# Two merges' gate projections by Strassen's block product, with the operand sums made on VectorE, ScalarE and GpSimd

## The chip, the cores and the metric

The kernel runs on one core of a Trainium2 chip. The core has a matrix engine (TensorE, PE in the rows, with its weight loads as PEld), VectorE (DVE), ScalarE (ACT), GpSimd (POOL) and SyncE (SP), each with its own in-order queue of instructions. The metric is the device time of one launch in microseconds (us); lower is better.

## The reference

One layer of a hybrid decoder block on x of 512 tokens by 1,024 channels, in float32. Four mixers read the same normalised input h; each result is projected and gated, and the four are summed:

```python
h = rmsnorm(x, norm_pre[l])
u = h @ w_in[l]                      # 1024 x 9,000-odd columns; the last 4096 are the merge gates
branches = (gdn_branch(...), gla_branch(...), ssd_branch(...), nsa_branch(...))
gates = jax.nn.sigmoid(_cols(u, offs, 'merge_gate', 'merge_gate')).reshape(bsz, s_len, 4, D_MODEL)
merged = jnp.zeros((bsz, s_len, D_MODEL), F32)
for n, y in enumerate(branches):
    merged = merged + gates[:, :, n] * (y @ w_br[l, n])
out = merged @ w_out[l]
x = x + rmsnorm(out, norm_post[l])
```

What matters here is `gates`: for each branch n, a product of a 1024x1024 weight with the transposed h (1024 channels by 512 tokens).

## The kernel before

**Products.** Every product is made of split operands: a float32 value is held as a high part and a low part (`hhi`/`hlo` for h, `wh`/`wl` for a weight, `yh`/`yl` for a branch's result), and `mm3` issues three matmuls for each block: wh with hhi, wh with hlo, wl with hhi. A weight tile of 128x1024 comes by DMA into `ws` (three buffers); ScalarE casts it into `wh`, VectorE subtracts `wl = ws - wh` (two buffers each). All of this is in `wload`.

**Stages.** The work is recorded stage by stage in the order of the list `ORDER`: the mixers `gdn`, `nsa`, `gla`, `ssd` and the merges `m0` (gdn), `m3` (nsa), `m1` (gla), `m2` (ssd). Then a list scheduler (`Sched`) places each recorded instruction on its engine's queue, by costs of its own and by free buffers of the pools (34 general buffers of 128x512 tagged `g`, 12 larger ones, 3 `ws`, 2 `wh`, 2 `wl`, 3 `mth` buffers, and in PSUM 3 banks `big` and 5 smaller uses). Stages overlap: products of the merge `m3` fill TensorE while the chains of the mixer `ssd` wait. All engine instructions are issued from one line (519), so rows are told apart by the names of their tiles.

**A merge.** `merge(n)` goes over four pairs of 128-channel blocks. A pair has two gate projections (`proj_ft`: 24 matmuls each of 128 weight rows by 512 tokens into one PSUM bank), then the branch's own product for the same two blocks (12 matmuls of 512 columns each). The gate goes through tanh on ScalarE into `mth`, VectorE forms (mth + 1) times the branch product in place, and GpSimd adds it to `merged`:

```python
th = S.buf("mth", [P, T], F32, 'cv')
act.activation(th, psg, AF.Tanh, scale=0.5)
...
dve.scalar_tensor_tensor(th, th, 1.0, ps, op0=OP.add, op1=OP.mult)
m_ops.append(pool.tensor_add(merged[d], merged[d], th))
```

**The end of `ssd`.** For each of four token tiles GpSimd adds the two parts of y (`y<-y,yo`), VectorE multiplies by the gate (`yz<-y,z`), ScalarE sums squares, VectorE and GpSimd make the reciprocal root (`yss`, `yrstd`), VectorE scales `yz` (`yz<-yz,yrstd,onc`), and TensorE transposes it with four matmuls `p_ssd<-ident,yz`. On TensorE these stand inside the products of `m3`, at places that the scheduler chose; TensorE's queue is in order, so a late `yz` holds up the products behind it.

After the merges `merged` is split into `hhi`/`hlo` once more and goes through `w_out` (matmuls `tf` of 256 columns, token rows out), the last norm and the residual.

Of the kernel before, what the change touches and what calls it, by code (L numbers as in the profile page):

```python
# [7 lines left out]
F32 = mybir.dt.float32  # L8
# [7 lines left out]
P = 128  # L16
# [25 lines left out]
NG = 34  # L42
N4 = 12
GPAIR = 0
ORDER = ('gdn', 'nsa', 'gla', 'm0', 'ssd', 'm3', 'm1', 'm2')

# [550 lines left out]
def block_kernel(ctx, tc, a, out):  # L599
# [131 lines left out]
    dskip = bcast_row('d_skip_c', 8)  # L731


    def wload(srcs, cut, shape, res=(), group=True):

        if group:
            S.grp += 1
        st, hi, lo = (S.buf(nm, [P, 1024], dt, nm).rearrange(cut, **shape)
                      for nm, dt in (('ws', F32), ('wh', F32R), ('wl', F32R)))
        o = 0  # L740
        for i, src in enumerate(srcs):
            n = src.shape[-1]
            op = sp.dma_start(st[:, :, o:o + n], src)
            if i == 0:
                op.resv = [v.buf for v in res]
            loads.append(op)
            o += n
        early = len(loads) <= 2
        S.urgent = 0 if early else -1
        c = act.copy(hi, st)  # L750
        t = (pool if early else dve).tensor_sub(lo, st, f32(hi))
        S.urgent = None
        if early:

            c.key, t.key = (0, xload.prio[1] + 40), (0, xload.prio[1] + 41)
        return hi, lo, op
# [926 lines left out]
            dve.scalar_tensor_tensor(z[c], opair, 0.5, z[c], op0=OP.mult, op1=OP.mult)  # L1683


    merged, m_ops = [None] * ND, []

    def merge(n):
        y = ytiles[n]
        yh, yl, ready = Feat("yh", F32R), Feat("yl", F32R), []  # L1690
        for b in range(4):
            ready.append(act.copy(yh[b], y[b]))
            ready.append(pool.tensor_sub(yl[b], y[b], f32(yh[b])))
        for d2 in range(ND // 2):
            ds = (2 * d2, 2 * d2 + 1)
            first = merged[ds[0]] is None
            if first:
                for d in ds:
                    merged[d] = w2("merged")
            ths = []  # L1700
            for i, d in enumerate(ds):
                psg = proj_ft(OFF['merge_gate'] + n * D + d * P, *([merged[v] for v in ds] if first and i == 0 else []),
                              group=i == 0)
                if i == 0:
                    for e in ready:
                        S.order(loads[-1], e)
                th = S.buf("mth", [P, T], F32, 'cv')
                act.activation(th, psg, AF.Tanh, scale=0.5)
                ths.append(th)
            src = a['w_br'][0, n][:, d2 * 256:(d2 + 1) * 256].rearrange("(b p) f -> p b f", p=P)  # L1710
            hi, lo, _ = wload([src], "p (b f) -> p b f", dict(f=256), group=False)
            for i, d in enumerate(ds):
                th = ths[i]
                ps = big()
                for b in range(4):
                    fs = slice(i * P, (i + 1) * P)
                    mm3(ps, hi[:, b, fs], lo[:, b, fs], yh[b], yl[b], b == 0, b == 3)
                if first:
                    dve.scalar_tensor_tensor(merged[d], th, 1.0, ps, op0=OP.add, op1=OP.mult)
                else:  # L1720
                    dve.scalar_tensor_tensor(th, th, 1.0, ps, op0=OP.add, op1=OP.mult)
                    m_ops.append(pool.tensor_add(merged[d], merged[d], th))

    stages = dict(gdn=gdn, nsa=nsa, ssd=ssd, gla=gla, m0=lambda: merge(0), m1=lambda: merge(1), m2=lambda: merge(2),
                  m3=lambda: merge(3))
    for i, stage in enumerate(ORDER):
        S.rank = i + 1
# [79 lines left out]
```

## Time and profile before

| | |
|---|---|
| median of 3 runs | 832.19 us (831.02 to 832.38) |
| the profiled execution: its time, its span | 830.03 us, 828.3 us |
| busy share: TensorE, VectorE, ScalarE, GpSimd | 97%, 60%, 45%, 25% |
| mean granted TensorE clock | 0.995 |

The span is the time from the first to the last instruction of the profiled execution; its device time is 1.73 us longer. Busy shares are shares of the span; a matmul's row has its own duration, and neighbouring matmuls overlap, so the step from one start to the next is what TensorE pays for one.

### The profile page before, as it was taken

To read this page: it belongs to the slowest core of one execution; us is meant where nothing else is said; L and a number is where in the kernel's file an instruction comes from. 1 tells how busy PE (TensorE), PEld (TensorE's weight loads), DVE (VectorE), ACT (ScalarE), POOL (GpSimd) and SP (SyncE) were. 2 spreads that over 40 slices of the span, in tenths; PEclk is the share of its full clock that TensorE was granted. 3 is DMA by queue.
4 is the path that set the end of the run, shared out by engine and by line. 5 is a ranking of instruction groups with operands and counts; after the bars stand their busy time and mean duration, and the time that the engine had idled before them with its cause. 6 is when DMAs were issued, how large, how long until landed. Compare 5 with 4: busy or idle time off the path is not lost.

```text
span 828.3 us, 12822 instructions
## 1 busy us (share of the span) xinstructions
PE 804.7 (97%) x4772; PEld 674.8 (81%) x4772; DVE 500.2 (60%) x1112; ACT 373.7 (45%) x878; POOL 204.7 (25%) x254
## 2 busy tenths in 40 slices
PE   5999999999999999999999899999999999999996
PEld 5888887897888899888887677898888888888996
DVE  5687766576535777777765977657633433343635
ACT  5444723323345767676554734635422222222432
POOL 6000263240231322222222500215521311121101
PEclk9999999999999999999999999999999999999998
DMA  7434254510132121211212221433133333334242
GB/s 231 89 104 127 77 135 104 128 27 2 51 102 76 52 53 52 77 52 51 77 51 77 52 77 51 115 105 100 51 102 87 92 102 102 81 98 127 94 162 102
DMA packets 112742, 72.39 MB, mean 87 GB/s; under 512 B 11788, under 2 KB 108232, under 8 KB 112680
## 3 DMA queue, kind: packets, MB, share of 16 engines
q1 hardware_dynamic: 111976, 69.86, 30.6%
q0 software_dynamic: 704, 1.70, 0.8%
q8 instruction: 38, 0.62, 0.3%
q14 instruction: 24, 0.20, 0.1%
HBM read 68.12 MB, written 3.43 MB: 86 GB/s over the span
## 4 chain that ended last, share of the span: by engine, by line
PE 88%; DVE 4%; ACT 2%; issue 2%; DMA 1%; POOL 1%; POOLq 0%; SPq 0%; DVEq 0%; ACTq 0%
PE big L519 58%; PE tf L519 11%; PE p_nsa L519 8%; PE p_gdn L519 5%; PE p_gla L519 2%; PE p_ssd L519 2%; DMA xt<-in_x 1%; DMA rows<-scrG 1%; PE p_head_tail L519 1%; DVE wl L519 0%; DVE gb L519 0%; POOL se L519 0%; ACT sq L519 0%; ACT wh L519 0%; DVE cv L519 0%
## 5 line engine op out<-in xcount | busy, mean ns | idle before, releaser
L519 DVE TENSOR_TENSOR wl<-ws,wh 128x1024 fp32r<-128x1024 f32 x108 | 147.9, 1369 | 161.3 <-ACT wh L519 160.1
L519 PE MATMUL big<-hlo,wh 128*128 128x512 f32 (+1 forms) x632 | 243.8, 393 | 0.0
L519 PE MATMUL big<-hhi,wh 128*128 128x512 f32 (+2 forms) x632 | 243.8, 393 | 0.0
L519 PE MATMUL big<-hhi,wl 128*128 128x512 f32 (+1 forms) x624 | 239.9, 392 | 0.0
L519 ACT CAST wh<-ws 128x1024 fp32r<-128x1024 f32 (+1 forms) x111 | 115.8, 1044 | 247.7 <-PE big L519 201.6
L519 PEld LDWEIGHTS big<-hhi,wh 128*128 128x128 f32 (+1 forms) x632 | 117.0, 188 | 25.6 <-issue 0.4
L519 PEld LDWEIGHTS big<-hlo,wh 128*128 128x128 f32 x632 | 116.3, 187 | 25.7 <-issue 0.6
L519 PEld LDWEIGHTS big<-hhi,wl 128*128 128x128 f32 x624 | 115.3, 188 | 25.1 <-issue 0.8
L519 PE MATMUL tf<-wl,hhi 128*128 128x256 f32 x288 | 81.0, 282 | 0.0
L519 PE MATMUL tf<-wh,hlo 128*128 128x256 f32 x288 | 80.9, 282 | 0.0
L519 PE MATMUL tf<-wh,hhi 128*128 128x256 f32 x288 | 80.9, 282 | 0.0
L519 POOL TENSOR_SCALAR se<-se,r,ngate 128x128 f32<-128x128 f32 (+1 forms) x64 | 41.5, 649 | 153.8 <-DVE r L519 121.0
L519 POOL TENSOR_TENSOR merged<-merged,mth 128x512 f32<-128x512 f32 x24 | 33.2, 1383 | 147.4 <-DVE mth L519 147.4
L519 PEld LDWEIGHTS tf<-wl,hhi 128*128 128x128 f32 x288 | 54.1, 188 | 0.4
L519 PEld LDWEIGHTS tf<-wh,hhi 128*128 128x128 f32 x288 | 54.0, 188 | 0.5
L519 PEld LDWEIGHTS tf<-wh,hlo 128*128 128x128 f32 x288 | 54.0, 188 | 0.4
L519 PE MATMUL big<-yl,wh 128*128 128x512 f32 x128 | 50.4, 394 | 0.0
L519 PE MATMUL big<-yh,wh 128*128 128x512 f32 x128 | 50.2, 392 | 0.0
L519 PE MATMUL big<-yh,wl 128*128 128x512 f32 x128 | 50.1, 392 | 0.0
L519 ACT ACTIVATE se<-se,mn 128x128 f32<-128x128 f32 (+1 forms) x64 | 36.1, 564 | 24.0 <-DVE mn L519 22.8
L519 DVE SCALAR_TENSOR_TENSOR cv<-big,cols,cv 128x511 f32<-128x511 f32 (+2 forms) x60 | 44.6, 743 | 1.5 <-ACT cv L519 0.5
L519 DVE CUSTOM_DVE_ANT_0 se<-p_nsa,nb 128x128 f32<-128x128 f32 (+1 forms) x64 | 30.9, 482 | 8.2 <-PE p_nsa L519 7.8
(335 smaller groups left out, 1240.4 us busy)
## 6 DMA issues: line engine op xcount, KB each, us to landing
ws<-in_w_in SPq DMA_DIRECT2D x84, 512.0 KB, 3.8
ws<-in_w_br SPq DMA_DIRECT2D x16, 512.0 KB, 3.5
ws<-in_w_out SPq DMA_DIRECT2D x8, 512.0 KB, 3.5
rows<-scrG SPq DMA_DIRECT2D x12, 256.0 KB, 4.8
xt<-in_x SPq DMA_DIRECT2D x4, 512.0 KB, 3.5
xr<-in_x SPq DMA_DIRECT2D x4, 512.0 KB, 4.4
out<-xo SPq DMA_DIRECT2D x8, 256.0 KB, 2.7
scrA<-B POOLq DMA_DIRECT2D x4, 256.0 KB, 3.1
```

Of the source, the lines that this page charges most:

```text
L519: return fn(*[res(v) for v in args], **{k: res(v) for k, v in kw.items()})
```

## The change

Between `m3` and `m1` a new stage `sums` is recorded; `m1` and `m2` then make the gate projections of a pair in `gate_pair`, in place of two calls of `proj_ft`. The weight of a pair is seen as two by two blocks A (two blocks of 128 gate channels, two halves of the 1024 input channels), h as two by two blocks B (two halves of the input channels, two halves of the 512 tokens). Strassen's form (in Winograd's variant) needs seven block products in place of eight:

- A11·B11, A12·B21, S1·T1, S2·T2, S3·T3, S4·B22 and A22·T4, each of 4 x 3 matmuls of 256 columns: 84 matmuls of 256 columns in place of 48 of 512.
- The sums S1 to S4 of weight blocks are made in each pair (four VectorE instructions of 128x512), and each of the seven left operands is split by a cast (ScalarE) and a subtraction (VectorE) of 128x512.
- The sums T1 to T4 of h are made once, in `sums`: for each of two groups four GpSimd additions `hx<-hhi,hlo`, four VectorE subtractions among the `hx`, four ScalarE casts and four VectorE subtractions for the low parts. T3 is written over the quarter of `hhi`/`hlo` that it replaces, so it waits for the last product of `m3`.
- The results are put together from two PSUM banks `fa` and `fb` with a copy `p15` (ScalarE, 128x512 from PSUM) and five VectorE additions of 256 columns; the second block of the tanh is taken in halves.

The branch's weight is cast and split in two halves. The loads are the same three of 512 KB per pair. `m0` and `m3` stay as they were.

```diff
...
-ORDER = ('gdn', 'nsa', 'gla', 'm0', 'ssd', 'm3', 'm1', 'm2')
+ORDER = ('gdn', 'nsa', 'gla', 'm0', 'ssd', 'm3', 'sums', 'm1', 'm2')
...
     dskip = bcast_row('d_skip_c', 8)
-    def wload(srcs, cut, shape, res=(), group=True):
+    def wload(srcs, cut, shape, res=(), group=True, halves=False):
...
             o += n
         early = len(loads) <= 2
         S.urgent = 0 if early else -1
-        c = act.copy(hi, st)
-        t = (pool if early else dve).tensor_sub(lo, st, f32(hi))
+        na = hi.arr.shape[0]
+        for r in ([slice(0, na // 2), slice(na // 2, na)] if halves else [slice(0, na)]):
+            c = act.copy(hi[:, r], st[:, r])
+            t = (pool if early else dve).tensor_sub(lo[:, r], st[:, r], f32(hi[:, r]))
         S.urgent = None
         if early:
...
             dve.scalar_tensor_tensor(z[c], opair, 0.5, z[c], op0=OP.mult, op1=OP.mult)
+    HT = T // 2
+    mov, sum_ops = {}, []
+    def sums():
+        c1, c2 = slice(0, HT), slice(HT, T)
+        ts = {n: [w2(f"T{n}{p}", None, F32R).rearrange("p (a b) -> p a b", b=HT) for p in "hl" for _ in range(2)]
+              for n in (1, 2, 4)}
+        for j in range(2):
+            k1, k2 = slice(2 * j, 2 * j + 2), slice(4 + 2 * j, 6 + 2 * j)
+            x11, x12, x21, x22 = (w2("hx").rearrange("p (a b) -> p a b", b=HT) for _ in range(4))
+            for x, k, c in ((x12, k1, c2), (x11, k1, c1), (x22, k2, c2), (x21, k2, c1)):
+                S.order(pool.tensor_add(x, f32(hhi[:, k, c]), f32(hlo[:, k, c])), loads[-7])
+            dve.tensor_sub(x11, x12, x11)
+            dve.tensor_sub(x12, x22, x12)
+            dve.tensor_sub(x22, x22, x11)
+            dve.tensor_sub(x21, x21, x22)
+            for n, x in ((1, x11), (2, x22), (4, x21), (3, x12)):
+                hi, lo = (ts[n][j], ts[n][2 + j]) if n != 3 else (hhi[:, k1, c2], hlo[:, k1, c2])
+                act.copy(hi, x)
+                sum_ops.append(dve.tensor_sub(lo, x, f32(hi)))
+        for n in (1, 2, 4):
+            mov['T', n] = [(ts[n][k // 2][:, k % 2], ts[n][2 + k // 2][:, k % 2]) for k in range(4)]
+        for n, k0, c in ((11, 0, c1), (21, 4, c1), (22, 4, c2)):
+            mov['B', n] = [(hhi[:, k0 + k, c], hlo[:, k0 + k, c]) for k in range(4)]
+        mov['T', 3] = [(hhi[:, k, c2], hlo[:, k, c2]) for k in range(4)]
+    def gate_pair(c0, res):
+        S.grp += 1
+        ws = []
+        s1, s2, s3, s4 = (w2(f"S{i}") for i in range(1, 5))
+        p15, u23 = w2("p15"), w2("u23")
+        for i in range(2):
+            st = S.buf("ws", [P, 1024], F32, 'ws')
+            op = sp.dma_start(st.rearrange("p (a f) -> p a f", f=P),
+                              W[:, c0 + i * P:c0 + (i + 1) * P].rearrange("(a p) f -> p a f", p=P))
+            if i == 0:
+                op.resv = [v.buf for v in (*res, s1, s2, s3, s4, p15, u23)]
+                for e in sum_ops:
+                    S.order(op, e)
+            loads.append(op)
+            ws.append(st)
+        first_load = loads[-2]
+        h1, h2 = slice(0, 512), slice(512, 1024)
+        a11, a12, a21, a22 = ws[0][:, h1], ws[0][:, h2], ws[1][:, h1], ws[1][:, h2]
+        S.urgent = -1
+        dve.tensor_add(s1, a21, a22)
+        dve.tensor_sub(s2, s1, a11)
+        dve.tensor_sub(s3, a11, a21)
+        dve.tensor_sub(s4, a12, s2)
+        S.urgent = None
+        parts = {}
+        for pair in ((('A', 11, a11), ('S', 1, s1)), (('S', 2, s2), ('A', 12, a12)), (('S', 3, s3), ('S', 4, s4)),
+                     (('A', 22, a22),)):
+            hi, lo = (S.buf(nm, [P, 1024], F32R, nm) for nm in ('wh', 'wl'))
+            for i, (nm, n, src) in enumerate(pair):
+                r = slice(i * 512, i * 512 + 512)
+                S.urgent = -1
+                act.copy(hi[:, r], src)
+                dve.tensor_sub(lo[:, r], src, f32(hi[:, r]))
+                S.urgent = None
+                parts[nm, n] = [v[:, r].rearrange("p (a f) -> p a f", f=P) for v in (hi, lo)]
+        fa, fb = big(), big()
+        l, r = slice(0, HT), slice(HT, T)
+        def product(ps, a_, b_, start):
+            (hi, lo), ms = parts[a_], mov[b_]
+            for k in range(4):
+                mm3(ps, hi[:, k], lo[:, k], *ms[k], start and k == 0, k == 3, True)
+        th1, th2 = (S.buf("mth", [P, T], F32, 'cv') for _ in range(2))
+        product(fa[:, l], ('A', 11), ('B', 11), True)
+        product(fa[:, r], ('S', 1), ('T', 1), False)
+        act.copy(p15, fa)
+        product(fb[:, l], ('S', 2), ('T', 2), True)
+        dve.tensor_add(u23[:, l], fb[:, l], p15[:, l])
+        product(fa[:, l], ('A', 12), ('B', 21), False)
+        product(fb[:, l], ('S', 3), ('T', 3), False)
+        dve.tensor_add(u23[:, r], fb[:, l], p15[:, l])
+        product(fa[:, r], ('S', 4), ('B', 22), False)
+        act.activation(th1[:, l], fa[:, l], AF.Tanh, scale=0.5)
+        dve.tensor_add(th1[:, r], fa[:, r], u23[:, l])
+        act.activation(th1[:, r], th1[:, r], AF.Tanh, scale=0.5)
+        product(fb[:, l], ('A', 22), ('T', 4), False)
+        dve.tensor_add(th2[:, l], fb[:, l], p15[:, l])
+        dve.tensor_add(th2[:, r], u23[:, r], p15[:, r])
+        act.activation(th2, th2, AF.Tanh, scale=0.5)
+        return [th1, th2], first_load
     merged, m_ops = [None] * ND, []
     def merge(n):
...
                 for d in ds:
                     merged[d] = w2("merged")
             ths = []
-            for i, d in enumerate(ds):
-                psg = proj_ft(OFF['merge_gate'] + n * D + d * P, *([merged[v] for v in ds] if first and i == 0 else []),
-                              group=i == 0)
-                if i == 0:
-                    for e in ready:
-                        S.order(loads[-1], e)
-                th = S.buf("mth", [P, T], F32, 'cv')
-                act.activation(th, psg, AF.Tanh, scale=0.5)
-                ths.append(th)
+            if mov:
+                ths, ld = gate_pair(OFF['merge_gate'] + n * D + d2 * 256, [merged[v] for v in ds] if first else ())
+                for e in ready:
+                    S.order(ld, e)
+            else:
+                for i, d in enumerate(ds):
+                    psg = proj_ft(OFF['merge_gate'] + n * D + d * P, *([merged[v] for v in ds] if first and i == 0 else []),
+                                  group=i == 0)
+                    if i == 0:
+                        for e in ready:
+                            S.order(loads[-1], e)
+                    th = S.buf("mth", [P, T], F32, 'cv')
+                    act.activation(th, psg, AF.Tanh, scale=0.5)
+                    ths.append(th)
             src = a['w_br'][0, n][:, d2 * 256:(d2 + 1) * 256].rearrange("(b p) f -> p b f", p=P)
-            hi, lo, _ = wload([src], "p (b f) -> p b f", dict(f=256), group=False)
+            hi, lo, _ = wload([src], "p (b f) -> p b f", dict(f=256), group=False, halves=bool(mov))
             for i, d in enumerate(ds):
                 th = ths[i]
                 ps = big()
...
                     dve.scalar_tensor_tensor(th, th, 1.0, ps, op0=OP.add, op1=OP.mult)
                     m_ops.append(pool.tensor_add(merged[d], merged[d], th))
-    stages = dict(gdn=gdn, nsa=nsa, ssd=ssd, gla=gla, m0=lambda: merge(0), m1=lambda: merge(1), m2=lambda: merge(2),
+    stages = dict(gdn=gdn, nsa=nsa, ssd=ssd, gla=gla, sums=sums, m0=lambda: merge(0), m1=lambda: merge(1), m2=lambda: merge(2),
                   m3=lambda: merge(3))
     for i, stage in enumerate(ORDER):
         S.rank = i + 1
```

On VectorE, at the end of `ssd` (names as above; `T1l` is the low part of T1; rows that begin with + are new):

```order
 L519 TENSOR_SCALAR yss<-yss 128x1
 L519 SCALAR_TENSOR_TENSOR rows<-rows,cb 128x512
+L519 TENSOR_TENSOR hx<-hx 128x512
+L519 SCALAR_TENSOR_TENSOR mth<-mth,big 128x512
 L519 SCALAR_TENSOR_TENSOR yz<-yz,yrstd,onc 128x512
+L519 TENSOR_TENSOR y<-p_ssd,xD 128x512
+L519 TENSOR_TENSOR hx<-hx 128x512 x2
+L519 SCALAR_TENSOR_TENSOR yo<-p_ssd,egc 128x512
+L519 TENSOR_TENSOR hx<-hx 128x512
+L519 TENSOR_TENSOR T1l<-hx,T1h 128x512
 L519 SCALAR_TENSOR_TENSOR mth<-mth,big 128x512
```

The fourth tile's `yz<-y,z` comes next but one behind these rows, then `T2l`, `T4l`, `yss`, two more `hx`, and the scaled `yz`; before, no `hx` and no `T` stood between. On TensorE the four transposes of that last `yz` stood behind 19 matmuls of the second last gate of their pair, and now stand behind six of the gate after it.

On GpSimd at the same place (`yl` is the low part of the nsa and ssd results, `yrstd` the reciprocal root):

```order
-L519 TENSOR_TENSOR yl<-z,yh 128x512 x2
+L519 TENSOR_TENSOR hx<-hhi,hlo 128x512 x2
 L519 TENSOR_TENSOR y<-y,yo 128x512
+L519 TENSOR_TENSOR hx<-hhi,hlo 128x512 x3
 L519 TENSOR_TENSOR yrstd<-yss,negh 128x1
+L519 TENSOR_TENSOR hx<-hhi,hlo 128x512
 L519 TENSOR_TENSOR merged<-merged,mth 128x512
+L519 TENSOR_TENSOR hx<-hhi,hlo 128x512
 L519 TENSOR_TENSOR y<-y,yo 128x512
+L519 TENSOR_TENSOR hx<-hhi,hlo 128x512
 L519 TENSOR_TENSOR merged<-merged,mth 128x512
```

Eight additions came in; the two `yl` moved behind the second `merged`.

On ScalarE in a pair of `m1` of the changed kernel (`S_6640` to `S_6643` are S1 to S4 of one pair, `p_6644` is `p15`):

```order
+L519 CAST wh<-S_6640 128x512
+L519 ACTIVATE mth<-mth 128x512
+L519 CAST wh<-S_6641 128x512
+L519 CAST wh<-ws 128x512
+L519 CAST wh<-S_6642 128x512
+L519 CAST wh<-S_6643 128x512
+L519 COPY p_6644<-big 128x512
+L519 CAST wh<-ws 128x512 x3
+L519 ACTIVATE mth<-big 128x256
```

Before, a pair had three casts of 128x1024 and two tanh of 128x512; the copy `p15` now stands behind the casts of S3 and S4.

## Rows read from the trace of the kernel before

**Rows 1.** The page: busy time of the engines, and the chain by engine.

```profile
PE 804.7 (97%) x4772; PEld 674.8 (81%) x4772; DVE 500.2 (60%) x1112; ACT 373.7 (45%) x878; POOL 204.7 (25%) x254
...
PE 88%; DVE 4%; ACT 2%; issue 2%; DMA 1%; POOL 1%; POOLq 0%; SPq 0%; DVEq 0%; ACTq 0%
```

**Rows 2.** Stretch, us: busy time of PE, PEld, DVE, ACT, POOL, clock.

```profile
650.00:700.00 50.00, 50.00 (x218) 40.47 (x217) 18.55 (x16) 12.43 (x16) 7.71 (x6) 1.00 0.35 95
```

**Rows 3.** Timeline of PE: start us, duration us; a pair of `m2`.

```profile
742.91 0.39 PE L519 MATMUL big<-hhi,wh 128*128 128x512 f32 x1
...
754.11 0.39 PE L519 MATMUL big<-yh,wh 128*128 128x512 f32 x1
...
759.57 0.39 PE L519 MATMUL big<-hhi,wh 128*128 128x512 f32 x1
```

**Rows 4.** Timeline of PE: matmuls of 256 columns.

```profile
18.30 1.07 PE L519 MATMUL big<-hhi,wl 128*128 128x256 f32 x8
20.11 1.07 PE L519 MATMUL big<-hlo,wh 128*128 128x256 f32 x8
...
779.76 0.28 PE L519 MATMUL tf<-wh,hhi 128*128 128x256 f32 x1
...
794.72 0.28 PE L519 MATMUL tf<-wl,hhi 128*128 128x256 f32 x1
```

**Rows 5.** Timeline of ACT: casts behind each other.

```profile
766.58 3.67 ACT L519 CAST hhi<-merged 128x512 fp32r<-128x512 f32 x6
775.86 0.62 ACT L519 CAST hhi<-merged 128x512 fp32r<-128x512 f32 x1 [3.58 <-POOL merged L519]
776.39 1.05 ACT L519 CAST wh<-ws 128x1024 fp32r<-128x1024 f32 x1
```

**Rows 6.** Groups by form: busy us, mean ns of one, idle before.

```profile
L519 ACT ACTIVATE mth<-big 128x512 f32<-128x512 f32 x32 | 18.9, 591 | 0.0
L519 DVE TENSOR_TENSOR hlo<-merged,hhi 128x512 fp32r<-128x512 f32 x8 | 5.1, 681 | 0.0
```

**Rows 7.** Timeline of DVE and POOL where they meet, and DVE alone.

```profile
605.21 1.23 DVE L519 TENSOR_TENSOR wl<-ws,wh 128x1024 fp32r<-128x1024 f32 x1 [3.99 <-ACT wh L519]
...
610.68 2.35 DVE L519 TENSOR_TENSOR wl<-ws,wh 128x1024 fp32r<-128x1024 f32 x1
610.67 1.29 POOL L519 TENSOR_TENSOR merged<-merged,mth 128x512 f32<-128x512 f32 x1 [1.50 <-DVE mth L519]
...
593.11 1.23 DVE L519 TENSOR_TENSOR wl<-ws,wh 128x1024 fp32r<-128x1024 f32 x1
593.17 2.32 POOL L519 TENSOR_TENSOR merged<-merged,mth 128x512 f32<-128x512 f32 x1 [1.40 <-DVE mth L519]
...
573.04 1.04 POOL L519 TENSOR_TENSOR xdd<-xdt,eld 128x512 f32<-128x512 f32 x1
573.45 1.18 DVE L519 TENSOR_TENSOR yz<-y,z 128x512 f32<-128x512 f32 x1
```

**Rows 8.** Timelines at the end of `ssd`: POOL, DVE, PE.

```profile
581.45 1.29 POOL L519 TENSOR_TENSOR y<-y,yo 128x512 f32<-128x512 f32 x1
...
583.14 0.68 DVE L519 TENSOR_TENSOR yz<-y,z 128x512 f32<-128x512 f32 x1
...
592.05 0.39 PE L519 MATMUL big<-hhi,wh 128*128 128x512 f32 x1
...
596.25 0.40 PE L519 MATMUL big<-hhi,wh 128*128 128x512 f32 x1
596.93 0.63 PE L519 MATMUL p_ssd<-ident,yz 128*128 128x128 f32 x4 [0.29 <-DVE yz L519]
```

**Rows 9.** PE at a gap, and the granted clock (PEclk) behind it.

```profile
474.09 0.49 PE L519 MATMUL p_gla<-qe,ke 64*128 64x128 f32 x4 [2.47 <-DVE ke L519]
...
476.00:477.00 1.00, 1.00 (x8) 0.41 (x8) 1.00 (x3) 0.75 (x2) 0.00 (x0) 0.50 0.00 0
479.00:480.00 1.00, 1.00 (x5) 0.75 (x4) 0.92 (x2) 0.95 (x2) 0.00 (x0) 0.97 0.55 137
```

## The prediction

> **What bounds the kernel now.** I read the page first: TensorE is busy 97% of the span, and the chain of work that ended last runs over TensorE for 88% of it [rows 1]. Then the windows by stage: in the merges after `ssd` TensorE is busy 50.00 of 50 us at a clock of 1.00, while VectorE works 18.55, ScalarE 12.43 and GpSimd 7.71 us [rows 2]. So there a microsecond of matmuls removed is a microsecond won, as long as the three helpers, with 30 us and more to spare in 50, deliver in time. The timeline of one pair of blocks gives the price: 48 gate matmuls of 512 columns from 742.91 to 754.11, 11.20 us or 233.3 ns each, then 24 of the branch to 759.57, 5.46 us; a pair is 16.66 us [rows 3]. `m1` and `m2` have eight such pairs.
>
> **The matmuls.** A pair's gates become 84 matmuls of 256 columns. That is 7/8 of the columns, but in 1.75 times the instructions, so the step of a 256-column matmul decides; break-even is 11.20/84 = 133 ns. Two places show steps: 16 matmuls from 18.30 to 20.11, 113 ns, and 127 steps from 779.76 to 794.72, 117.8 ns [rows 4]. Their weights change with each matmul, as here. I take half the gate's step, 116.7 ns, which lies between: a product of 12 is 1.40 us, seven are 9.80, and the raw gain is 1.40 us a pair (1.30 by the slower row, 1.68 by the faster).
>
> The Trainium skill ("TensorE: Matmul & The Clock Gate", Back-to-back issue gap) states 262 cycles at 2.4 GHz for 256 columns and 518 for 512, 109 and 216 ns; by it seven products would be an estimated 9.2 us. The 233.3 ns of the trace speak against using it here, since a gate's matmul takes 17 ns longer than that.
>
> **A pair's helpers.** VectorE gets four S sums, seven low parts and two halves of the branch's low part, 13 of 128x512 at 0.68 us [rows 6], 8.9 us; five additions of 256 columns (between half of 0.68 and all of it, about 0.45 each) 2.2 us; and the two products with mth as before, about 1.4 us: 12.5 us in a pair of about 15.7. ScalarE gets nine casts, the copy and tanh: about 8 us (casts 0.61, tanh 0.59 [rows 5, 6]). Both fit on the average; what matters is order. In ScalarE's queue the copy p15 stands behind the casts of S3 and S4, and these need a `wh` buffer (there are two) that S1·T1 is still reading. Call X the end of S1·T1. The two casts and the copy end 0.05 + 2 x 0.53 + 0.6 = 1.73 us after X if casts follow each other as at 775.86 and 776.39, and 1.9 us if as the six from 766.58, 3.67 us together [rows 5]. A12·B21 adds into the half of the bank that p15 reads, so it can't start before; its nominal start is X + 1.40. TensorE waits 0.37 to 0.55 us in each pair; I take 0.4. What comes late next is S3·T3, with operands cast long before, so nothing builds up. The weight loads are the same three per pair, and earlier than needed. The period is then 9.80 + 0.40 + 5.46 = 15.66 us, a gain of 1.0 us a pair, **8.0 us** for eight (7.2 by the slower step of rows 4, 10.4 by the faster without change of the wait).
>
> **Entry to m1.** The first pair has no pair ahead to hide behind: its four sums stand on VectorE behind the last-but-one `mth` product of `m3`, which needs half of the branch products, 2.7 us after the last gate of `m3` ends, and 0.2 more, and then three instructions and the split of A11 follow, partly against a GpSimd addition. I count VectorE done at 7.1 us after that gate, and TensorE through the branch products at 5.5 to 5.9: **1.5 us** lost (0 to 2.5).
>
> **The sums.** This term decides the sign. `sums` puts eight GpSimd additions, eight VectorE subtractions, eight casts and eight more subtractions beside the end of `ssd`. None of them is on TensorE, and VectorE and GpSimd have idle time there. But the rows show that the two don't work beside each other. The split `wl` takes 1.23 us alone and 2.35 us when it starts 0.01 us behind a GpSimd addition of 1.29 us; the same addition started 0.06 us behind a `wl` takes 2.32; `yz<-y,z` takes 1.18 beside `xdd` and 0.68 alone [rows 7, 8]. In each case the later one ends a full instruction behind the end of the earlier: 0.55 us for a VectorE instruction of 128x512, 1.08 for one of 1024, 1.15 for the GpSimd addition. So instructions of both with operands in SBUF go one by one, in turns. All sixteen VectorE instructions of `sums` and all eight additions are of that kind.
>
> The Trainium skill ("SBUF — State Buffer", Who interferes with whom) has this as a rule: a VectorE instruction with two inputs in SBUF shares a read port with GpSimd, and whoever issues first holds it to its end. By that rule the sums aren't hidden but queue up; the trace agrees, 2.35 us against 1.23.
>
> Now the queues as the change orders them. GpSimd's eight additions stand ahead of the second `merged`, six of them behind the `y` that starts at 581.45 and ends at 582.75 [rows 8]. From there to the last scaled `yz` the exclusive work is: on GpSimd six additions, one y and two merged, 9 x 1.15 = 10.4 us; on VectorE 15 instructions of 128x512 (among them nine of `sums`), 8.3 us, and two `wl`, 2.2 us. That is 20.9 us, so `yz` can't be done before 603.7. VectorE's four instructions that read PSUM (4 x 0.6 us) need no turn but hold their queue, and GpSimd's `yrstd` stands between VectorE's `yss` and the scaled `yz`; stepping through both queues in turns these add some 4 us, and I get 607.7. Before, `yz` let TensorE go on at 596.93, after a wait of 0.29 us [rows 8].
>
> TensorE reaches these transposes later than before in the program: six matmuls into the next gate. Its own way there is already held up twice (`rows` is late by 1.9 and 1.1 us, since it waits in VectorE's queue, and the third tile's `yz` by 1.1, partly overlapping), so the gate that began at 592.05 [rows 8] starts at about 594.3, and the transposes are reached at 601.3. They wait until 607.7: 6.4 us. Before, the same place in the program was passed at about 600.0; after, at 608.2. **8.2 us late**, with 4 (if `yz` is done at 603.7) and 10 as bounds.
>
> A wait of that length costs the clock too. The one comparable gap of the trace, 2.47 us of idle TensorE up to 474.09, is followed by a granted clock at half of 2.4 GHz (0.50) in three slices of 1 us from 476 on, and part of a fourth, back to 0.97 at 479 to 480 [rows 9]. About 3.4 us at half speed cost **1.7 us** (0 if the gap is short).
>
> The casts and low parts of T3 come after the last gate of `m3` and are counted in the entry. The end of the kernel is as before.
>
> **Sum.** Against the profiled execution of before, 830.03 us: + 8.2 + 1.7 + 1.5 - 8.0 = 833.4. The median of the runs stands 2.16 us higher (832.19), so I forecast **835.6 us**. A difference of 0.2%, 1.7 us, is about what a measurement of this kernel can tell from no change.
>
> **Rivals.**
> *The sums hide after all* (faster). If GpSimd's additions run early, in the gaps that it has before 581.45, or if the yz chain gets ahead of them, TensorE isn't held and only the entry is lost: 832.19 + 1.5 - 8.0 = 825.7. It decides where `yz` is ready by 601.3. For it speak GpSimd's idle time; against it that its queue is in order, and all eight additions stand behind `ssd`'s own instructions, six of them behind the y of 581.45 [rows 8]. Chance 0.22.
> *Half of it* (same). The wait is 3 to 4 us, the clock is kept or half lost: 832.19 + 4 + 0.8 + 1.5 - 8.0 = 830.5, up to 833.8. Chance 0.23.
> *VectorE becomes the bound of a pair* (slower than forecast). 12.5 us and two additions of GpSimd that lock it out, 2 x 1.29, are 15.1 of 15.7; with the waits for ScalarE between, a pair could last 16.2. The gain is then 3.7 and the time 839.9. For it speaks the alternation; against it that half of VectorE's work is needed only late in a pair. Chance 0.13.
> *256 columns cost 133 ns or more*, so that Strassen saves nothing: 843.6. No row shows such a step. Chance 0.02.
> The forecast has the remaining 0.40.
>
> **Range.** From 826.0 to 840.5. Below lies the better half of the first rival; above, the bound of 10 us together with the slower step, and what is worse than 839.9 in the third: together under 0.2. By themselves the forecast's own bounds are 831 to 839. Faster by over 0.2% are the first rival and a little of the second, 0.25; within 0.2% most of the second and a little of the forecast, 0.21; slower the rest, 0.54.
>
> **What the changed profile would show.** The gate stretch of a pair at 9.8 us for 84 matmuls, steps near 117 ns, and a pair at 15.7; a wait of 0.4 us ahead of A12·B21 that ends with p15; at the end of `ssd` VectorE and GpSimd instructions of 128x512 at up to twice their length, a TensorE wait of some 6 us released by VectorE's `yz`, and PEclk at 0.5 for some 3 us behind it; a wait of about 1.5 us ahead of the first A11·B11. The prediction is wrong if `yz` comes early (no long wait), if a pair's period isn't near 15.7, or if the transposes stand elsewhere than at the place where TensorE comes first.

## The result, and the profile after

The changed kernel takes 837.9 us (median of 4 runs, 837.52 to 839.0) against 832.08 us: a ratio of 1.0085 (95% interval 1.0071 to 1.0100; the two medians alone give 1.0070). The forecast of 835.6 us lies 2.3 us below; its direction held, its size didn't. The profiled execution took 837.55 us, 7.5 us more than that of before, where the forecast had 3.4. The page's line of busy times and the chain by engine:

```profile
PE 800.5 (96%) x5060; PEld 685.9 (82%) x5060; DVE 574.9 (69%) x1248; ACT 401.0 (48%) x950; POOL 224.0 (27%) x262
...
PE 82%; DVE 10%; ACT 3%; issue 2%; DMA 1%; POOL 1%; POOLq 0%; DVEq 0%; SPq 0%; ACTq 0%
```

TensorE is busy 4 us less than before [rows 1], in a span 7.5 us longer: matmuls were saved, and more than that was lost in waits. The chain now runs over VectorE for 10%. What TensorE waited for from 560 to 790 us (engine and tile, releaser: us in all, times, longest):

```profile
PE p_ssd L519 <- DVE yz L519: 5.4, 1, 5.4
PE big L519 <- DVE wl L519: 3.3, 1, 3.3
PE p_ssd L519 <- issue: 2.4, 3, 1.4
PE big L519 <- ACT p L519: 1.5, 7, 0.2
```

Three places, then: the last `yz` of `ssd`, the first low part `wl` of m1, and the copy `p15` in seven of the eight pairs. The three waits put down to the issue (2.4 us) stand ahead of the products `p_ssd<-xdt,rows` of `ssd`; one of 0.7 was there before. First the end of `ssd`, in the timelines of GpSimd, VectorE and TensorE (start us, duration us):

```profile
582.01 4.65 POOL L519 TENSOR_TENSOR hx<-hhi,hlo 128x512 f32<-128x512 f32 x3
...
582.45 1.41 DVE L519 TENSOR_TENSOR yz<-y,z 128x512 f32<-128x512 f32 x1
583.78 1.76 DVE L519 SCALAR_TENSOR_TENSOR rows<-rows,cb 128x512 f32<-128x512 f32 x1
585.46 2.28 DVE L519 TENSOR_TENSOR wl<-ws,wh 128x1024 fp32r<-128x1024 f32 x1
...
604.50 1.75 DVE L519 SCALAR_TENSOR_TENSOR yz<-yz,yrstd,onc 128x512 f32<-128x512 f32 x1
...
606.39 1.09 PE L519 MATMUL p_ssd<-ident,yz 128*128 128x128 f32 x4 [5.44 <-DVE yz L519]
...
608.13 0.63 PE L519 MATMUL big<-hhi,wl 128*128 128x512 f32 x1
608.56 0.63 PE L519 MATMUL big<-hhi,wh 128*128 128x512 f32 x1
...
611.04 0.39 PE L519 MATMUL big<-hlo,wh 128*128 128x512 f32 x1
```

GpSimd's three `hx` take 4.65 us, 1.55 each, and beside them `yz` takes 1.41, `rows` 1.76 and `wl` 2.28 us; alone, `yz` took 0.68 and `wl` 1.23 [rows 7, 8]. The last scaled `yz` is done at 606.25; TensorE waits 5.44 us for it, and then takes 0.43 us from one matmul of 512 columns to the next until 0.23 returns. The windows show why (us, then busy time of PE, PEld, DVE, ACT and POOL; the number behind POOL's count is the granted clock):

```profile
604.00:605.00 1.00, 0.00 (x0) 0.00 (x0) 1.00 (x2) 1.00 (x2) 1.00 (x2) 0.50 0.00 0
609.00:610.00 1.00, 1.00 (x4) 0.81 (x3) 1.00 (x2) 0.72 (x2) 1.00 (x1) 0.50 0.76 199
610.00:611.00 1.00, 1.00 (x5) 0.82 (x4) 1.00 (x2) 0.00 (x0) 1.00 (x2) 0.79 0.92 324
```

Within the wait the granted clock falls to 0.50, and it comes back only behind 610. TensorE reaches m1 at 651.68, against 642.95 before. All work of this run stood 0.69 us earlier than in the run of before when `ssd` came to its last steps, so the loss there is 9.4 us. The rows for this are two of the kernel before and one of the changed kernel:

```profile
576.18 1.97 PE L519 MATMUL p_ssd<-xdt,rows 128*128 128x64 f32 x16 [0.67 <-issue]
642.95 0.39 PE L519 MATMUL big<-hhi,wh 128*128 128x512 f32 x1
...
575.49 1.97 PE L519 MATMUL p_ssd<-xdt,rows 128*128 128x64 f32 x16 [0.68 <-issue]
```

Then the entry to m1, the same three engines:

```profile
650.00 1.67 POOL L519 TENSOR_TENSOR merged<-merged,mth 128x512 f32<-128x512 f32 x1 [12.65 <-DVE mth L519]
651.63 3.38 POOL L519 TENSOR_TENSOR yl<-yT,yh 128x512 fp32r<-128x512 f32 x2
...
649.23 0.69 DVE L519 SCALAR_TENSOR_TENSOR mth<-mth,big 128x512 f32<-128x512 f32 x1 [4.27 <-PE big L519]
649.84 2.38 DVE L519 TENSOR_TENSOR S<-ws 128x512 f32<-128x512 f32 x2
652.15 1.75 DVE L519 TENSOR_TENSOR S<-S,ws 128x512 f32<-128x512 f32 x1
653.81 1.75 DVE L519 TENSOR_TENSOR wl<-ws,wh 128x512 fp32r<-128x512 f32 x1
...
651.68 0.28 PE L519 MATMUL big<-hhi,wh 128*128 128x256 f32 x1
...
655.62 0.58 PE L519 MATMUL big<-hhi,wl 128*128 128x256 f32 x1 [3.30 <-DVE wl L519]
...
661.54 0.32 PE L519 MATMUL big<-T2l,wh 128*128 128x256 f32 x1
...
673.42 0.28 PE L519 MATMUL big<-hhi,wh 128*128 128x256 f32 x1
```

The weight sums S stand behind `mth`, start at 649.84, and meet three GpSimd additions in a row: `merged` and two `yl`. The third sum and the first `wl` behind it take 1.75 us each instead of 0.7. TensorE begins m1 at 651.68, issues four matmuls, waits 3.30 us, and then goes at half clock, 0.21 us a matmul of 256 columns, until 661.54. The first pair lasts to 673.42, 21.74 us.

The other seven pairs, here the last:

```profile
767.97 0.28 PE L519 MATMUL big<-hhi,wh 128*128 128x256 f32 x1
...
772.63 0.38 PE L519 MATMUL big<-hhi,wh 128*128 128x256 f32 x1 [0.21 <-ACT p L519]
...
778.24 0.40 PE L519 MATMUL big<-yh,wh 128*128 128x512 f32 x1
...
783.74 0.28 PE L519 MATMUL tf<-wh,hhi 128*128 128x256 f32 x1
```

From 767.97 to 778.24 the gates take 10.27 us. The last matmul ahead of the gap started at 772.13, 0.50 us before that of 772.63, so 0.38 us of this are the wait and the 84 matmuls took 9.89; with the branch a pair takes 15.77 us. Before it took 16.66 [rows 3].

### The profile page after: what moved, and what is told of

It reads as the page before. It is cut to its first block, busy times and chain, and to the rows that moved or that the text cites. A ratio compares the mean times of both kernels' runs of the same rounds, so it can differ in the third digit from the quotient of the medians.

```text
span 835.8 us, 13677 instructions
## 1 busy us (share of the span) xinstructions
PE 800.5 (96%) x5060; PEld 685.9 (82%) x5060; DVE 574.9 (69%) x1248; ACT 401.0 (48%) x950; POOL 224.0 (27%) x262
## 4 chain that ended last, share of the span: by engine, by line
PE 82%; DVE 10%; ACT 3%; issue 2%; DMA 1%; POOL 1%; POOLq 0%; DVEq 0%; SPq 0%; ACTq 0%
PE big L519 52%; PE tf L519 11%; PE p_nsa L519 8%; PE p_gdn L519 5%; DVE wl L519 3%; PE p_gla L519 2%; PE p_ssd L519 2%; DVE mth L519 1%; ACT wh L519 1%; DMA xt<-in_x 1%; DVE yz L519 1%; DVE hx L519 1%; PE p_head_tail L519 1%; DMA rows<-scrG 1%; DVE S L519 0%
## 5 line engine op out<-in xcount | busy, mean ns | idle before, releaser
L519 PE MATMUL big<-hhi,wh 128*128 128x512 f32 (+2 forms) x632 | 231.5, 374 | 1.6 <-ACT p L519 1.5
L519 PE MATMUL big<-hlo,wh 128*128 128x512 f32 (+1 forms) x632 | 229.5, 371 | 0.0
L519 PE MATMUL big<-hhi,wl 128*128 128x512 f32 (+1 forms) x624 | 225.8, 369 | 3.3 <-DVE wl L519 3.3
L519 DVE TENSOR_TENSOR wl<-ws,wh 128x1024 fp32r<-128x1024 f32 (+1 forms) x124 | 146.8, 1190 | 104.6 <-ACT wh L519 104.3
L519 ACT CAST wh<-ws 128x1024 fp32r<-128x1024 f32 (+2 forms) x127 | 114.6, 909 | 173.3 <-PE big L519 125.7
L519 POOL TENSOR_TENSOR merged<-merged,mth 128x512 f32<-128x512 f32 x24 | 36.3, 1525 | 139.6 <-ACT mth L519 90.1
```

The lines of the kernel that those rows point to most:

```text
L519: return fn(*[res(v) for v in args], **{k: res(v) for k, v in kw.items()})
```

## The experiments

All ratios are to the kernel before, run on the same chip beside them. Since the work ahead of the sums ended 0.7 us earlier to 1.8 us later than in the run of before, the loss at the end of `ssd` is counted from a row that they all have (the sixteen matmuls `p_ssd<-xdt,rows` at 575 to 578 us) to the first matmul of m1, less the same of before: 9.4 us for the changed kernel. Each experiment has one trace, and the executions of one kernel lie up to 6 us apart (830.76 to 836.94 in the ten of VectorE's sums held back). This stretch, left as it was, lost 9.4 us in the changed kernel, 9.8 in "weight sums first" and 10.1 in "the copy sooner"; differences of that size between two traces show nothing.

My theory at this point: VectorE and GpSimd go in turns, so the sums hold up the `yz` chain; the entry is held by the place of the weight sums in VectorE's queue; the pairs by the place of `p15` in ScalarE's. The rivals: queue length alone at the end of `ssd`; a late weight load at the entry; VectorE's subtractions in a pair.

**GpSimd writes only.**

```diff
-                S.order(pool.tensor_add(x, f32(hhi[:, k, c]), f32(hlo[:, k, c])), loads[-7])
+                S.order(pool.memset(x, 0.5, _r=[f32(hhi[:, k, c]), f32(hlo[:, k, c])]), loads[-7])
+                S.ops[-1].cost = 1227.0
+                pool.memset(x, 0.5)
+                S.ops[-1].cost = 1.0
```

> The changed kernel with each of the eight GpSimd additions hx = hhi + hlo replaced by two writes of a constant into the same buffer, about as long together, which read nothing from SBUF; so the T sums are not those of h. The order on TensorE, VectorE and ScalarE is the same to the row. Theory (VectorE and GpSimd go in turns when both read SBUF): the VectorE instructions beside the writes take 0.68 us instead of 1.4 to 1.8, the last scaled yz is done some 6 us sooner, TensorE's wait of 5.4 us ahead of the last transposes falls below 1.5 us and the half clock behind it goes; the time falls from 837.6 by 7 to 9 us, to about 829 to 831. Rival (the queues are simply too long: nine more VectorE instructions ahead of yz, and GpSimd as busy as before): yz comes at most 2 us sooner and the time stays above 835.

Measured: ratio 1.0040 (1.0023 to 1.0057), profiled execution 834.56 us, 3.0 less than the changed kernel's. GpSimd, VectorE and TensorE at the end of `ssd`:

```profile
582.61 3.10 POOL L519 MEMSET hx<- 128x512 f32 x6
...
583.29 0.68 DVE L519 TENSOR_TENSOR yz<-y,z 128x512 f32<-128x512 f32 x1
584.63 1.23 DVE L519 TENSOR_TENSOR wl<-ws,wh 128x1024 fp32r<-128x1024 f32 x1
...
595.76 1.77 DVE L519 TENSOR_TENSOR yz<-y,z 128x512 f32<-128x512 f32 x1
...
601.24 1.76 DVE L519 SCALAR_TENSOR_TENSOR yz<-yz,yrstd,onc 128x512 f32<-128x512 f32 x1
...
603.14 1.09 PE L519 MATMUL p_ssd<-ident,yz 128*128 128x128 f32 x4 [3.79 <-DVE yz L519]
```

Beside the six writes from 582.61 the first `yz` and `wl` take what they take alone, though GpSimd is busy without a break there. So the doubling comes from two engines reading, not from GpSimd being busy; that part of the theory holds. The Trainium skill ("SBUF — State Buffer", Who interferes with whom) draws the same line: a VectorE instruction with two inputs in SBUF contends with a GpSimd instruction that reads SBUF, not with one that only writes it; 0.68 us beside the writes agrees. But only 3 us came back, and 6.1 of the 9.4 us stay: the wait is still 3.79 us, and the half clock is there. The expectation failed, and the run doesn't separate queue length from turns, since GpSimd's own `merged`, `y` and `yl` still read: from 589 to 603 us six VectorE rows, the last two `yz` among them, take some 5 us more than alone. Two of these GpSimd instructions are the `yl<-z,yh` that the change moved from 579 us to a place beside `T2l` and the last `yz`; no run puts them back.

**VectorE's sums held back**, the counterpart (run later, shown here): the GpSimd additions as they are, the subtractions behind the last `yz`.

```diff
-            dve.tensor_sub(x11, x12, x11)
+            S.order(dve.tensor_sub(x11, x12, x11), loads[-4])
```

> The changed kernel with the GpSimd additions where they are (same rows, same order up to the second merged) but VectorE's subtractions among the hx, and so the T parts, held back to loads[-4], behind the last yz. The counterpart to the run in which GpSimd only wrote: there 4.1 of some 10 us by which yz was late came back. Theory (both halves count: GpSimd's reads, and nine more instructions in VectorE's queue): the GpSimd additions alone still make VectorE's own yz, rows and wl wait their turn, some 2 to 4 us of the 9.5 stay, time 831 to 834 against 837.6, with rows of 1.2 to 1.8 us on VectorE beside hx. Rival (VectorE's own queue is all that counts): the wait ahead of the last transposes is under 0.5 us and TensorE reaches m1 as early as without sums, time below 829.5.

Measured: ratio 1.0035 (1.0018 to 1.0052), profiled execution with 5.6 of the 9.4 us still lost. VectorE, then TensorE:

```profile
583.02 1.41 DVE L519 TENSOR_TENSOR yz<-y,z 128x512 f32<-128x512 f32 x1
...
596.63 2.31 DVE L519 TENSOR_TENSOR wl<-ws,wh 128x1024 fp32r<-128x1024 f32 x1
...
601.55 0.63 PE L519 MATMUL p_ssd<-ident,yz 128*128 128x128 f32 x4 [1.99 <-DVE yz L519]
...
602.92 0.63 PE L519 MATMUL big<-hlo,wh 128*128 128x512 f32 x1
```

VectorE's own `yz` and `wl` still wait their turn (1.41, 2.31 us). The loss that stays is more than the expected 2 to 4 us, though the median, 833.64 us, lies in the range that was named, and the rival (below 829.5) falls: 5.6 us are lost here without any of VectorE's sums. So with either half gone 5.6 to 6.1 us stay in the trace, of 9.4; each pays for the clock: after a wait of only 1.99 us the matmuls take 0.43 us as well, from 602.49 to 605.90. Whether the two halves add isn't shown: the traces give back 3.3 and 3.8 us, together less than 9.4, but by the ratios it is 3.7 and 4.2 us, each within some 2 us, together no less than the 7.3 us that moving both brings (below).

**No sums.** The seven products read blocks of h in place of T1 to T4.

```diff
     def sums():
         c1, c2 = slice(0, HT), slice(HT, T)
+        for n, k0, c in ((1, 0, c2), (2, 4, c2), (3, 0, c2), (4, 4, c1)):
+            mov['T', n] = [(hhi[:, k0 + k, c], hlo[:, k0 + k, c]) for k in range(4)]
...
+        return
```

> The changed kernel without the stage sums: the seven products read blocks of h in place of T1 to T4, so the gates are not the reference's; matmuls, weight sums and the putting together stay. Theory: the loss at the end of ssd (9.5 us by comparing when TensorE reaches m1) goes, the pairs keep 15.76 us against 16.66, and the entry to m1 keeps part of its 6.0 us: 837.6 - 9.5 = 828 if the entry is unchanged, 825 if the entry shrinks with the earlier load. Rival (the sums matter little and the pairs themselves don't gain): not below 832.

Measured: ratio 0.9926 (0.9906 to 0.9947), profiled execution 822.97 us, median 825.13. TensorE reaches m1 as in the kernel before (within 0.1 us), a pair takes 15.7 us, and the entry has no wait at all: the load is no longer ordered behind T3, and the sums S begin at 634.34, 9.4 us ahead of m1's first matmul. That is the lower of the two expected times: part of the entry's cost is the sums' too. The rival falls.

**Sums only**, with the gates of m1 and m2 plain.

```diff
-            if mov:
+            if False:
...
-            hi, lo, _ = wload([src], "p (b f) -> p b f", dict(f=256), group=False, halves=bool(mov))
+            hi, lo, _ = wload([src], "p (b f) -> p b f", dict(f=256), group=False, halves=False)
```

> The changed kernel with the gates of m1 and m2 plain again (two proj_ft per pair) but with the stage sums, whose T1, T2 and T4 nobody reads; since T3 is written over a quarter of h, the gates of m1 and m2 are not the reference's. It prices the sums by themselves. Theory (all of the 9.5 us at the end of ssd is the sums' own): slower than before by 9 to 10 us, ratio 1.0105 to 1.012, with a TensorE wait of over 5 us ahead of the last transposes. Rival (part of that loss comes from the Strassen pairs, whose loads and buffers reach back into m3): at most 5 us slower.

Measured: ratio 1.0126 (1.0111 to 1.0141), 10.5 us and so a little above what was expected; 10.1 of them lie at the end of `ssd`. The wait ahead of the last transposes was 3.9 us (expected over 5), the rest shorter waits ahead of it and the half clock, here twice: from 588 to 596 us already, behind a wait of 1.36 us, and again behind the long wait. The sums' price is their own, and the rival falls.

**Weight sums first.** The last two `mth` products of m3 are ordered behind S4 of the first pair.

```diff
-        dve.tensor_sub(s4, a12, s2)
+        o4 = dve.tensor_sub(s4, a12, s2)
+        if res_first[0]:
+            res_first[0] = False
+            for e in stts[-2:]:
+                S.order(e, o4)
...
-                    dve.scalar_tensor_tensor(th, th, 1.0, ps, op0=OP.add, op1=OP.mult)
+                    stts.append(dve.scalar_tensor_tensor(th, th, 1.0, ps, op0=OP.add, op1=OP.mult))
```

> The changed kernel, with the two last products mth of m3 on VectorE held back behind the weight sums S1 to S4 of the first pair of m1 (and so their GpSimd additions). Theory (the entry costs 6.0 us since the sums stand behind mth, which waits for TensorE, and then meet GpSimd's additions): the sums run about 3 us sooner and alone, the wait of 3.3 us ahead of the second half of A11 B11 falls below 0.5 us, the clock stays whole there, and the time falls by 4 to 6 us to about 832 to 833.5. Rival (the weight load comes too late, so the place in the queue does not matter): less than 1.5 us.

Measured: ratio 1.0045 (1.0029 to 1.0061), profiled execution 833.58 us, 4.0 less than the changed kernel's, at the edge of what was expected; the median of its five runs is 835.24. VectorE at the entry, where m1 begins at 652.57:

```profile
645.77 1.29 DVE L519 TENSOR_TENSOR S<-ws 128x512 f32<-128x512 f32 x2
646.97 0.69 DVE L519 TENSOR_TENSOR S<-S,ws 128x512 f32<-128x512 f32 x1
648.51 0.69 DVE L519 TENSOR_TENSOR wl<-ws,wh 128x512 fp32r<-128x512 f32 x1 [0.85 <-ACT wh L519]
```

The sums now begin 6.8 us ahead of m1's first matmul instead of 1.8, and take some 0.65 us each; so the load wasn't late, and the rival falls. They start earlier and also meet no GpSimd addition; the run takes both away at once. What TensorE waited for that it had not waited for in the changed kernel:

```profile
PE big L519 <- DVE u L519: 0.8, 1, 0.8
PE big L519 <- DVE mth L519: 0.3, 1, 0.3
```

The wait for `wl` is gone, and the clock stays at 1.00; 1.1 us of new waits (for the addition u23 and for `mth`) take its place, and the first pair takes 16.9 us instead of 21.7.

**The copy sooner.**

```diff
+        S.urgent = -2
         act.copy(p15, fa)
+        S.urgent = None
```

> The changed kernel with ScalarE's copy p15 ahead of the cast of S4 instead of behind it, nothing else moved but the addition that reads it. Theory (TensorE waits 0.38 us in each pair for that copy, which stands behind two casts): the copy ends 0.5 us sooner, the wait goes, a pair falls from 15.76 to about 15.4 us and the time by 2.5 to 3 us to about 834.8. Rival (VectorE's subtractions are what a pair waits for next): the period stays above 15.65 and the time falls by less than 1 us.

Measured: ratio 1.0045 (1.0029 to 1.0061), profiled execution 835.37 us, median 835.14. TensorE at the end of `ssd`, then the last pair:

```profile
587.77 1.08 PE L519 MATMUL p_ssd<-xdt,rows 128*128 128x64 f32 x8 [1.36 <-issue]
...
766.31 0.28 PE L519 MATMUL big<-hhi,wh 128*128 128x256 f32 x1
...
781.57 0.28 PE L519 MATMUL tf<-wh,hhi 128*128 128x256 f32 x1
```

A pair takes 15.26 us, 0.5 less than without the edit; the wait for `p15` is gone from TensorE's list. The rival falls: VectorE is not what a pair waits for. From m1's first matmul to the end of m2 TensorE takes 4.9 us less; the profiled time falls by only 2.2, since this execution stood 2.1 us later when `ssd` came to its last steps and lost 0.6 more there. Behind the wait of 1.36 us at 587.77 the granted clock fell to 0.50 from 589 to 596, which it did not in the changed kernel behind 1.37 us at the same place.

**Sums later.**

```diff
-                S.order(pool.tensor_add(x, f32(hhi[:, k, c]), f32(hlo[:, k, c])), loads[-7])
+                S.order(pool.tensor_add(x, f32(hhi[:, k, c]), f32(hlo[:, k, c])), loads[-4])
```

> The changed kernel with the GpSimd additions held back until a load three further in m3 (loads[-4] in place of loads[-7]), nothing else. The sums then run beside the last pairs of m3, where VectorE works about 37% and GpSimd 15% of the time, behind the last yz. Theory (the sums cost because they stand ahead of the yz chain on VectorE and GpSimd; the pairs of m3 can hide them): the wait of 5.4 us and the half clock behind it go, the time falls by 8 to 10 us to 828 to 829.5, the entry to m1 still costs about 6 us. Rival (16 VectorE and 8 GpSimd instructions in turns can't be hidden anywhere in m3, and hold up its wl): TensorE waits for wl in m3 and less than 4 us come back.

Measured: ratio 0.9997 (0.9988 to 1.0007), median 830.65 us; no measurable difference from the kernel before, and 1.2 us short of the expected 828 to 829.5. TensorE's waits:

```profile
PE big L519 <- DVE wl L519: 4.4, 2, 3.2
PE p_ssd L519 <- DVE yz L519: 0.3, 1, 0.3
```

The wait for `yz` is back to what it was [rows 8]; of the 9.4 us 1.4 stay, for a `wl` of m3 that now waits beside the sums (1.2 us). The entry still waits 3.2.

**All three**, with the sums at `loads[-4]`, and then at three other places. The edit is that of the three runs above together.

> All three repairs at once: sums held back to loads[-4], the weight sums of the first pair ahead of the last two mth products of m3, p15 ahead of the cast of S4. By the terms measured apart (9.5 + 4.0 + 3): 837.6 - 16 = about 821.5, ratio to the kernel before 0.989 to 0.991. If the terms cover one another (the later sums press on the entry): 824 to 827.

Measured: ratio **0.9916** (0.9900 to 0.9933), median 823.58 us, 7 us faster than the kernel before. TensorE's waits, now 2.0 us for `wl` and `u` together:

```profile
PE big L519 <- DVE wl L519: 1.2, 1, 1.2
PE big L519 <- DVE u L519: 0.8, 1, 0.8
```

> As the run with loads[-4], with the sums one load later still (loads[-3]). Theory (m3's last two pairs have room for them): within 1 us of it. Rival (they now end too late for the first products of m1): slower than it by 2 us or more, with a TensorE wait at the entry to m1.

Measured: 0.9932 (0.9917 to 0.9947), 1.3 us slower than with `loads[-4]`, so neither within 1 us nor 2 us off; TensorE's waits for `wl` are 1.8 instead of 1.2 us, and those for `mth` 1.3 instead of 0.3.

> As the kernel with all three repairs and loads[-4] (ratio 0.9916 to the kernel before), with the sums one load earlier (loads[-5]). There TensorE still waited 1.2 us for a wl in m3, beside the sums, and 1.1 us in the first pair of m1. Theory (the m3 wait comes from the sums' place in VectorE's queue ahead of that wl): it moves with the sums; if the new place has no wl behind it the time falls by about 1.5 us, ratio 0.990; otherwise the ratio is 0.9905 to 0.993. It is slower than 0.994 only if the sums reach back into the yz chain.

Measured: 0.9961 (0.9946 to 0.9975), beyond the 0.994 that I had set as the limit, and for another reason than the one named: the `yz` chain isn't touched. VectorE, then TensorE:

```profile
603.85 5.16 DVE L519 TENSOR_TENSOR hx<-hx 128x512 f32<-128x512 f32 x3 [2.42 <-POOL hx L519]
...
610.64 2.28 DVE L519 TENSOR_TENSOR wl<-ws,wh 128x1024 fp32r<-128x1024 f32 x1
...
612.98 0.79 PE L519 MATMUL big<-hhi,wl 128*128 128x512 f32 x1 [2.51 <-DVE wl L519]
```

Four VectorE instructions of the sums, some 1.7 us each beside seven GpSimd additions, stand ahead of a `wl` of m3, and TensorE waits 2.51 us for it. The matmul behind the gap takes 0.79 us instead of 0.39, so the clock fell here too.

> As the one before with loads[-6]: two of the GpSimd additions now stand ahead of the second merged, and one hx and nothing else of VectorE's sums ahead of the last yz. Theory (only what stands ahead of yz costs): yz is late by 1 to 2.5 us, which the wait of m3 no longer adds to, ratio 0.990 to 0.994. Rival (half the sums' cost is back): 0.996 or more.

Measured: 0.9955 (0.9939 to 0.9971), between the two expectations: 1.7 us of waiting for `yz`, and 1.8 us for a `wl`. Of the four places `loads[-4]` is the cheapest, and one load to either side costs 1.3 or 3.7 us: in these traces the cost went with what stands behind the sums in VectorE's queue and how soon TensorE needs it.

## Why the prediction was right in kind and wrong in size

By its own terms, against the profiled executions (+7.5 us measured, +3.4 forecast; against the medians the miss is smaller, 2.3 us and not 4.1, since the profiled execution of the changed kernel lay 0.35 us below its median and that of before 2.16):

- **The sums at the end of `ssd`: 8.2 + 1.7 = 9.9 us forecast, 9.4 measured.** The place (the last four transposes), the releaser (`yz`), the turns and the half clock behind were as forecast. `yz` was done at 606.25, 1.45 us sooner than I had, half of that since the whole run stood 0.69 us earlier; the waits for `rows` that I put at 1.9 and 1.1 us were 1.37 and 0.35. The prediction's one sum of both queues holds several things: nine VectorE instructions of the sums, the eight GpSimd additions, and the turns of each with what stood there before. Taking away either the additions' reads or VectorE's sums leaves 5.6 to 6.1 us, as the two counterpart runs show.
- **The matmuls and the wait in a pair: 15.66 us forecast, 15.76 measured.** The wait for `p15` is 0.38 us (0.4 forecast; the two queue times named, less 1.40, give 0.33 to 0.5 and not 0.37 to 0.55). The step is 117.7 ns, the slower of the two rows and not half the gate's 233.3: 9.89 us for 84, where I had 9.80. With the copy sooner the gates did take 9.80. Over eight pairs this is 0.8 us.
- **The entry to m1: 1.5 us forecast (0 to 2.5), 6.0 measured.** This is the step that failed. It was 4.5 us short, and the whole sum 4.1 (837.55 against 833.4): the pairs add 0.8, the end of `ssd` takes back 0.5, and 0.7 is how much earlier this run stood ahead of the sums. I had VectorE done 7.1 us after the last gate, "partly against a GpSimd addition": a single one. There were three. The two splits `yl` of the `ssd` result stand next in GpSimd's queue, as they did before, and VectorE's sums, which weren't there before, fall beside them; three of the four VectorE instructions waited a turn of about 1.1 us: VectorE was done at 655.56, 9.3 us after the last gate ended at 646.22. And I charged a long wait with the clock at the end of `ssd`, but not here: 28 matmuls from 655.62 to 661.71 take 6.1 us where 3.3 would do, 2.8 us. So 3.5 us of wait and 2.8 of clock (less 0.4, since this pair has no wait for `p15`), against 1.5 and none. The run with the weight sums first takes that wait and that clock away at once. The casts and low parts of T3, which I had after the last gate and counted in here, were done at 644.96, while that gate still ran.
- **The rivals.** The sums didn't hide where they stood, though nearly all of them hide three loads later. The wait was 5.44 us and not the 3 to 4 of *Half of it*. VectorE didn't become the bound of a pair. The step of 256 columns stayed well below 133 ns.

So the change gains nearly what it promised in the pairs (0.9 us each of 1.0, 1.4 with the copy in its place), and gives it back twice at their borders, where the one-time sums and the first pair's sums meet other work on VectorE and GpSimd. Runs that take each away show it: the sums (9.4 us, by leaving them out, keeping them alone, and moving them), the entry (4.0), the copy (0.5 us a pair). How the 9.4 us split between turns, queue, the displaced `yl` and clock stays open.

## What to carry to other kernels

When work is moved from the engine that bounds to engines with idle time, walk the queues at the borders of the stage, not its steady state: here the steady pairs were forecast within 0.1 us and the one entry was off by 4.5. List the VectorE instructions with all operands in SBUF and the GpSimd instructions that read SBUF in that stretch as one single queue, and look for what the change has pushed into it. Every wait of 1.99 us or more on TensorE that these runs had at these places was followed by a stretch at half clock, so such a wait is charged with that too. Shorter waits differ: two of 1.36 us were each followed by such a stretch, and one of 1.37 at the same place was not.

## What the runs showed of the hardware that wasn't expected

- The clock's price did not follow the length of the wait: behind waits of 1.99, 3.79 and 5.44 us (in three kernels, at the same place) the matmuls of 512 columns went at 0.43 us a step instead of 0.23, until 0.23 came back 4.4, 5.9 and 4.2 us after the wait's end; that cost some 1.6, 2.6 and 1.9 us. A shorter wait saved its own length and hardly anything of the clock.
- Taking one of two causes of a wait away brought back 3.3 (the reads of the GpSimd additions) or 3.8 us (VectorE's sums) of 9.4 in one trace each; leaving out both brought all.
- The step of a matmul of 256 columns went by the product: in the last pair 119 ns in S2·T2 (770.82 to 772.13) and 113 ns in A12·B21 from 773.07 on, though both are the same form. It isn't the wait between them: with the copy sooner, and no wait, the two products took 120 and 113 ns. There the 84 took 9.80 us instead of 9.89, about what the slower step right behind the wait (772.63 to 772.85) costs. The runs don't say why the products differ.
